# Row-wise value products for the second query block, a masked level and a halved last tile in a two-layer hybrid trunk

## The chip, the cores and the metric

The kernel runs on one core of one Trainium2 chip. A core has five engines: TensorE (PE, the matrix products; its weight loads are shown as PEld), VectorE (DVE), ScalarE (ACT), GpSimd (POOL) and SyncE (SP, which here issues the DMAs). The metric is device time in microseconds; times are medians of several runs, and a profile is one execution of its own.

## The reference

Two layers of a decoder trunk on 512 tokens of 1024 features in float32. In each layer one projection feeds four groups of four heads of 64 features:

```python
h = _rmsnorm(x, norm_g[l])
(...) = jnp.split(h @ w_in[l], split_at, axis=-1)
y = concatenate([hgrn2_mixer(...),          # gated linear recurrence, chunkwise
                 fox_mixer(...),            # softmax(q.k/8 + sums of log f), causal
                 stick_breaking_mixer(...), # A[t,s] = beta[t,s] prod(1 - beta[t,j])
                 nsa_mixer(...)])           # compressed + selected + window branch, gated
yh = y per head * rsqrt(mean(y*y) + EPS)
x = x + (yh * out_norm_g[l] * silu(gate)) @ w_out[l]
...
return _rmsnorm(x, final_norm_g)
```

In the attention groups a block of 128 queries sees the keys of its own and all earlier blocks, so query block 0 has one key block, block 1 two, block 3 four. In the first group, o[t] is a sum over s up to t of q[t] exp(b[t] - b[s]) k[s] v[s], with b the running sum of log f.

## The kernel before

All operations are recorded first (every instruction stands under the recorder's line, L484), then `Program.order` places them by a list schedule with its own costs, and they are issued in that order, one program for each engine. What sets the order are tables at the end of the file: `TIMES` (start and step of each of eight threads of work), `LEAD` and `LAG` (shifts of priority by buffer), `RESERVE` (buffers kept back), `FILL`. The engines then run their programs in order and wait for each other by semaphores.

PE's results go to four kinds of buffers: `pin` (4, projections), `pss` (2, scores and grams), `pso` (1, value products), `psm` (1, transposes of probabilities and small products).

Projections (`tproj`, `nproj`) split both operands into a high and a low part (`whi`, `wlo`, `hth`, `htl`) and add three products for each of eight chunks of 128 features, 512 output columns wide, into a `pin` buffer. They fill most of PE's time; the attention work is threaded between them.

Attention in `fox` and `stick` runs per pair of heads `i` and query block `qb`: scores, probabilities, `turned` (PE transposes them by blocks into `psm`, and VectorE or ScalarE copies them out). The value product has two forms. In the first block (`qb == 0`) it is made by rows: the turned probabilities (128 x 128) are the weights, the values (128 x 64) move, and the output already has queries on partitions. In later blocks it is a bundle (`together`, issued without anything in between) with the values as weights, the two heads on the two halves of the array, 128 probability columns moving; the output is by features, and `heads_back` copies it with ScalarE (`oT`) and transposes it back on PE. `attend` (the gated group) has only the second form, for all blocks, with two branches on the two halves and two heads moving (256 columns), and two transposes per pair. A PE product in float32 is two passes, and the trace shows each pass as a record.

The first group (`hgrn`) builds its matrix within a 128-row block by levels of width 1, 2, 4, 8, 16, 32, 64: VectorE, ScalarE and GpSimd make operand `G` (buffers `h4`, shown as `h_h`), PE makes 64 small products in one bundle per level (`gram`). Levels up to 8 multiply 32 x 32 squares, and VectorE copies the entries of that level under a mask (`copy_predicated`) into `A32`. Level 16 multiplies 16 x 16 squares, and ScalarE copies them into their place in `A32`, eight copies for each layer. GpSimd then copies `A32` into the full matrix `Ad`.

At the end `out_proj` makes the output tiles by 128 rows and halves of 512 columns, adds the old rows, and sums their squares; `final` computes the row scale (VectorE, then a power on GpSimd), scales the two halves on VectorE and ScalarE, and stores them. The last tile's second half is the last product on PE.

Of the kernel before, what the change touches and what calls it, by code (L numbers as in the profile page):

```python
# [12 lines left out]
F32 = mybir.dt.float32  # L13
# [14 lines left out]
NCMP = 31  # L28
SMALL = (8, 4, 2, 1)
O_HGQ, O_HGF, O_HGI = 0, 256, 512  # L30
# [517 lines left out]
def trunk(ctx: ExitStack, tc: tile.TileContext, cst, x, norm_g, w_in, lbl, fox_fb, pe_k, w1_k, w2_k,  # L548
# [99 lines left out]

    def nproj(w, n, tb):
        hi, lo = w  # L650
        ps = pin.tile([P, T], F32, name="pin", tag="pin")
        o = ps[:, :n]
        sl = slice(tb * P, (tb + 1) * P)
        for c in range(KC):
            pe.matmul(o, hth[:, c, sl], hi[c][:, :n], start=(c == 0), stop=False)
            pe.matmul(o, hth[:, c, sl], lo[c][:, :n], start=False, stop=False)
            pe.matmul(o, htl[:, c, sl], hi[c][:, :n], start=False, stop=(c == KC - 1))
        return o
# [124 lines left out]
    for l in range(nl):  # L783
# [257 lines left out]
        def hgrn():  # L1041
# [55 lines left out]
            for i in range(2):  # L1097
                state(i)
                yield
            for wv in SMALL[::-1] + (16, 32, 64):  # L1100
                G = h4.tile([P, 2, T], F32, name="hG", tag="h4")
# [81 lines left out]
        def fox(i):  # L1183
            need(("fx", i))
            Q1, Q2, K1, K2 = st["fx", i]
            for qb in range(NB):
# [32 lines left out]
        def stick(i):  # L1219
            need(("sb", i))  # L1220
            Q1, K1, K2 = st["sb", i]
            for qb in range(NB):
# [23 lines left out]
                po = pso.tile([P, P], F32, name="po", tag="pso")  # L1246
                if qb == 0:
                    pn = po.rearrange("p (h d) -> p h d", h=2)
                    for s in range(2):
                        pe.matmul(pn[:, s], aT[s][:, 0], bv[:, 0, 2 * i + s, :], start=True, stop=True)  # L1250
                else:
# [10 lines left out]
        def attend(qb):  # L1262
# [35 lines left out]
            for i in range(2):  # L1298
                us = {}
                for s in range(2):  # L1300
# [7 lines left out]
                    yield  # L1308
                po = pso.tile([P, 2, P], F32, name="po", tag="pso")
# [5 lines left out]
                with pr.together("pe", 0.5):  # L1315
                    for kb in range(qb + 1):
                        for br in range(2):
                            pe.matmul(po[64 * br:64 * br + 64], nv[:, kb, br, :], pT[kb][:, 2 * br:2 * br + 2],
                                      start=(kb == 0), stop=(kb == qb))
                oT = t2.tile([P, 2, P], F32, name="oT2", tag="k1", bufs=3)  # L1320
                act.activation(oT, po, AF.Copy)
                pn = pso.tile([P, 2, 2, HD], F32, name="pon", tag="pso")
                for s in range(2):
                    pe.transpose(pn[:, s], oT[:, s], ident)
                w = den[:, 1:3, 2 * i:2 * i + 2]
# [38 lines left out]
        def out_proj(w, tb, g):  # L1364
# [12 lines left out]
            if l < nl - 1:  # L1377
                wr[tb, g] = sp.dma_start(xdst[rs, cs], XY[:, tb, cs])

        def final(tb):  # L1380
# [60 lines left out]
        if not last:  # L1441
            w_hgi = wload(w_in[l + 1], [(O_HGI, 256, 0), (O_FXV, 256, 256)], 512)
        for tb in range(NB):
            out_proj(wo, tb, 1)
            if last:
# [10 lines left out]

TIMES = ((2.577, 1.29), (10.591, 0.713), (11.607, 0.725), (20.2, 0.497), (50.852, 0.974), (58.753, 0.235), (13.999, 1.112), (62.9, 0.953))
RESERVE = {'gp_G': 1, 'pin_pin': 2, 'sm_mr': 3, 't2_t2': 1, 'vp_vp': 3, 'psm_psm': 2, 'wp_whi': 2}
FILL = (0, 1, 2, 6, 3, 4, 5, 7)
LEAD = {'pin_pin': 20, 'psm_psm': -20, 'pss_pss': 10, 'qk_qk': 100, 'sm_mr': -80, 't2_k1': 120, 'vp_vp': -180, 'wp_wlo': 290, 'pa_junk': 0, 't2_t2': 0, 't2_oT': 40, 'gp_G': 10, 'pa_pa': 10, 'sm_nm': -10, 'one_htl': 100, 'one_hth': -20, 'wp_whi': 20}  # L1460
FULL = (128, 128)
# [36 lines left out]
```

## Time and profile before

| | us |
|---|---|
| median of 3 runs | 669.25 |
| lowest, highest | 668.04, 673.2 |
| the profiled execution | 669.13 |
| its span, first to last instruction | 667.3 |
| PE busy in it | 652.6 |
| VectorE, ScalarE, GpSimd busy | 464.8, 415.5, 149.8 |

The span is from the first to the last instruction; the time of the execution has 1.83 us around it. PE's granted clock is 0.995 of full speed over the span. Busy time of PE counts overlapping products as one stretch, so the distance between starts says more about what a product costs.

### The profile page before, as it was taken

How to read it: one execution, taken by the hardware profiler on the slowest of the kernel's cores; microseconds unless marked ns; L12 is line 12 of the kernel's file. 1: busy time of each engine (PE TensorE's matmuls, PEld its weight loads, DVE VectorE, ACT ScalarE, POOL GpSimd, SP SyncE). 2: the span in 40 equal slices, each digit the busy share in tenths (PEclk: the TensorE clock that was granted, in tenths of full speed). 3: DMA queues.
4: the chain of work that ended last, by engine and by line, in shares of the span. 5: the costliest groups of instructions: out<-in, count | busy, mean ns of one | idle time of the engine just before them, and what ended most of it. 6: DMA issues, size and time to landing. Idle time of an engine off the chain costs nothing.

```text
span 667.3 us, 13759 instructions
## 1 busy us (share of the span) xinstructions
PE 652.6 (98%) x5371; PEld 517.6 (78%) x5371; DVE 464.8 (70%) x968; ACT 415.5 (62%) x902; POOL 149.8 (22%) x173
## 2 busy tenths in 40 slices
PE   7999998999999999999999999999999999999996
PEld 4888986778887777777888898877788877787774
DVE  5646589667788968755672476976678898796553
ACT  5456356566766879765353655557587678886632
POOL 5000223312343313210000030350222332141000
PEclk8999999999999999999999999999999999999998
DMA  7544243451433204204352425337123411050022
GB/s 251 151 107 131 61 134 104 107 117 32 127 95 97 80 1 137 71 1 158 111 158 58 106 64 142 100 81 188 35 74 105 129 50 40 25 163 20 32 80 94
DMA packets 67161, 63.67 MB, mean 95 GB/s; under 512 B 20484, under 2 KB 51736, under 8 KB 67096
## 3 DMA queue, kind: packets, MB, share of 16 engines
q1 hardware_dynamic: 67096, 62.80, 33.1%
q8 instruction: 42, 0.69, 0.4%
q14 instruction: 23, 0.19, 0.1%
HBM read 52.79 MB, written 4.19 MB: 85 GB/s over the span
## 4 chain that ended last, share of the span: by engine, by line
PE 95%; issue 2%; DVE 1%; DMA 1%; ACT 0%; SPq 0%; POOLq 0%; POOL 0%; DVEq 0%
PE pin_pin L484 67%; PE pss_pss L484 13%; PE pso_pso L484 9%; PE psm_psm L484 7%; DMA one_XY<-in_x 1%; DVE sm_vcm L484 0%; DVE sm_K1c L484 0%; SPq L484 0%; ACT t_t L484 0%; DVE wp_wlo L484 0%; DVE h_h L484 0%; ACT pa_pa L484 0%; ACT h_h L484 0%; DVE one_XY L484 0%; POOLq L1494 0%
## 5 line engine op out<-in xcount | busy, mean ns | idle before, releaser
L484 PE MATMUL pin_pin<-wp_whi,one_hth 128*128 128x512 f32 (+1 forms) x384 | 151.9, 396 | 2.0 <-ACT wp_whi L484 2.0
L484 PE MATMUL pin_pin<-wp_wlo,one_hth 128*128 128x512 f32 (+1 forms) x384 | 151.4, 395 | 0.5 <-DVE wp_wlo L484 0.5
L484 PE MATMUL pin_pin<-wp_whi,one_htl 128*128 128x512 f32 (+1 forms) x384 | 151.0, 397 | 0.0
L484 DVE TENSOR_TENSOR wp_wlo<-wp_raw,wp_whi 128x1024 fp32r<-128x1024 f32 (+1 forms) x80 | 95.5, 1199 | 48.1 <-ACT wp_whi L484 47.9
L484 PE MATMUL pin_pin<-one_htl,wp_whi 128*128 128x512 f32 x256 | 103.0, 402 | 1.5 <-issue 1.5
L484 PE MATMUL pin_pin<-one_hth,wp_wlo 128*128 128x512 f32 x256 | 103.8, 405 | 0.0
L484 PE MATMUL pin_pin<-one_hth,wp_whi 128*128 128x512 f32 x256 | 102.8, 402 | 0.0
L484 ACT ACTIVATE wp_whi<-wp_raw 128x1024 fp32r<-128x1024 f32 (+1 forms) x80 | 82.7, 1038 | 29.8 <-PE pin_pin L484 22.7
L484 POOL TENSOR_TENSOR sm_rs<-sm_ssv,one_mhalf 128x2 f32<-128x2 f32 (+1 forms) x48 | 43.2, 901 | 204.6 <-DVE sm_ssv L484 200.6
L484 PEld LDWEIGHTS pin_pin<-wp_whi,one_hth 128*128 128x128 f32 x384 | 72.5, 189 | 13.8 <-ACT wp_whi L484 2.3
L484 PEld LDWEIGHTS pin_pin<-wp_whi,one_htl 128*128 128x128 f32 x384 | 72.5, 189 | 12.9 <-issue 1.5
L484 PEld LDWEIGHTS pin_pin<-wp_wlo,one_hth 128*128 128x128 f32 x384 | 72.7, 189 | 12.5 <-DVE wp_wlo L484 0.7
L484 PE MATMUL pss_pss<-qk_qk,qk_qk 128*128 128x512 f32 (+3 forms) x224 | 65.1, 376 | 0.0
L484 ACT ACTIVATE t_t<-pss_pss,sm_nm 128x128 f32<-128x128 f32 (+3 forms) x96 | 50.3, 527 | 21.2 <-DVE sm_nm L484 18.3
L484 PEld LDWEIGHTS pin_pin<-one_htl,wp_whi 128*128 128x128 f32 x256 | 48.1, 188 | 12.4 <-issue 2.4
L484 PEld LDWEIGHTS pin_pin<-one_hth,wp_wlo 128*128 128x128 f32 x256 | 48.2, 188 | 11.2 <-issue 1.1
L484 PEld LDWEIGHTS pin_pin<-one_hth,wp_whi 128*128 128x128 f32 x256 | 48.2, 188 | 10.1 <-issue 0.3
L484 ACT ACTIVATE pa_pa<-pa_pa 128x512 f32<-128x512 f32 (+4 forms) x90 | 50.8, 565 | 7.1 <-DVE pa_pa L484 5.7
L484 DVE TENSOR_REDUCE sm_nm<-pss_pss 128x1 f32<-128x384 f32 (+3 forms) x72 | 42.8, 597 | 16.7 <-PE pss_pss L484 16.1
L484 PE MATMUL psm_psm<-one_c_ident,t_t 128*128 128x128 f32 x320 | 53.5, 275 | 0.9 <-DVE sm_vcm L484 0.9
L484 POOL TENSOR_TENSOR h_h<-h_h,h_h 128x512 f32<-128x512 f32 (+1 forms) x16 | 26.2, 1641 | 118.0 <-ACT h_h L484 110.9
L484 ACT ACTIVATE t_t<-psm_psm 128x512 f32<-128x512 f32 (+3 forms) x72 | 38.7, 538 | 18.0 <-PE psm_psm L484 17.6
(183 smaller groups left out, 1047.7 us busy)
## 6 DMA issues: line engine op xcount, KB each, us to landing
wp_raw<-in_w_in SPq DMA_DIRECT2D x56, 256.0 KB, 3.4
wp_raw<-in_w_in SPq DMA_DIRECT2D x28, 512.0 KB, 3.7
wp_raw<-in_w_out SPq DMA_DIRECT2D x16, 512.0 KB, 3.6
qk_qk<-qk_qk SPq DMA_DIRECT2D x16, 256.0 KB, 3.4
one_XY<-in_x SPq DMA_DIRECT2D x4, 512.0 KB, 7.8
pa_pa<-in_x SPq DMA_DIRECT2D x8, 256.0 KB, 3.2
xres<-one_XY SPq DMA_DIRECT2D x8, 256.0 KB
pa_pa<-xres SPq DMA_DIRECT2D x8, 256.0 KB, 3.5
```

Of the source, the lines that this page charges most:

```text
L484: fn(*[r(a) for a in args], **{k: r(v) for k, v in kw.items()})
```

## The change

Five edits. In `fox` and `stick` the second query block (`qb == 1`) takes the row form too: four products of 64 columns (two heads, two key blocks) in place of a bundle of four, a ScalarE copy and a transpose. In `attend` the first block takes the row form: four products in place of a bundle of two, a ScalarE copy of 256 columns and two transposes. Level 16 joins the levels that multiply 32 x 32 squares and are copied under a mask; the eight ScalarE copies for each layer go, and two masked VectorE copies come. The last output tile's second half is made in two halves of 256 columns by a function of its own, `out_last`. The tables that set the order get other numbers.

```diff
-SMALL = (8, 4, 2, 1)
+SMALL = (16, 8, 4, 2, 1)
...
-            for wv in SMALL[::-1] + (16, 32, 64):
+            for wv in SMALL[::-1] + (32, 64):
...
-                for e, ps in enumerate(gram(G, G, wv if wv >= 16 else 0)):
-                    if wv >= 16:
+                for e, ps in enumerate(gram(G, G, wv if wv >= 32 else 0)):
+                    if wv >= 32:
                         for j in range(P // (2 * wv)):
                             rows_ = slice(2 * wv * j, 2 * wv * j + wv)
-                            dst = A32[e][rows_, :, 16:32] if wv == 16 else Ad[e][rows_, :, 2 * wv * j + wv:2 * wv * (j + 1)]
-                            act.activation(dst, ps[rows_], AF.Copy)
+                            act.activation(Ad[e][rows_, :, 2 * wv * j + wv:2 * wv * (j + 1)], ps[rows_], AF.Copy)
...
-                if qb == 0:
+                if qb < 2:
                     pn = po.rearrange("p (h d) -> p h d", h=2)
                     for s in range(2):
-                        pe.matmul(pn[:, s], pT[0, s], fv[:, 0, 2 * i + s, :], start=True, stop=True)
+                        for kb in range(qb + 1):
+                            pe.matmul(pn[:, s], pT[kb, s], fv[:, kb, 2 * i + s, :], start=(kb == 0), stop=(kb == qb))
...
+                if qb == 0:
+                    pn = pso.tile([P, 2, 2, HD], F32, name="pon", tag="pso")
+                    for s, br in itertools.product(range(2), range(2)):
+                        pe.matmul(pn[:, s, br], pT[0][:, 2 * br + s], nv[:, 0, br, :], start=True, stop=True)
+                else:
...
+        def out_last(w):
...
+            for u in range(2):
+                us, cs = slice(256 * u, 256 * u + 256), slice(512 + 256 * u, 768 + 256 * u)
+                dve.tensor_tensor(XY[:, tb, cs], nproj(w, 256, tb, 256 * u), old[:, us], OP.add)
+                act.activation(old[:, us], XY[:, tb, cs], AF.Square, accum_out=sq[:, u:u + 1])
+                dve.tensor_tensor(o[:, cs], XY[:, tb, cs], nxt["gb"][:, cs], OP.mult)
+                if u == 0:
+                    dve.tensor_tensor(sq[:, 2:3], sq[:, 0:1], part, OP.add)
+                    dve.tensor_scalar(sq[:, 2:3], sq[:, 2:3], 1.0 / D, EPS, op0=OP.mult, op1=OP.add)
+            dve.scalar_tensor_tensor(sq[:, 2:3], sq[:, 1:2], 1.0 / D, sq[:, 2:3], op0=OP.mult, op1=OP.add)
+            rsq(sq[:, 3:4], sq[:, 2:3], 1)
+            for us, e in ((slice(0, 640), dve), (slice(640, 1024), act)):
+                if e is act:
+                    act.activation(o[:, us], o[:, us], AF.Copy, scale=sq[:, 3:4])
+                else:
+                    dve.tensor_scalar(o[:, us], o[:, us], sq[:, 3:4], None, op0=OP.mult)
+                sp.dma_start(out[rs, us], o[:, us])
...
-RESERVE = {'gp_G': 1, 'pin_pin': 2, 'sm_mr': 3, 't2_t2': 1, 'vp_vp': 3, 'psm_psm': 2, 'wp_whi': 2}
+RESERVE = {'gp_G': 1, 'pin_pin': 2, 'sm_mr': 3, 't2_t2': 1, 'vp_vp': 1, 'psm_psm': 2, 'wp_whi': 2}
```

The same edit as in `fox` stands in `stick`, with `aT[s][:, kb]` and `bv`. `out_last(wo)` takes the place of `out_proj` and `final` for the last tile. In `TIMES`, `LEAD` and `RESERVE` six numbers differ and one is new.

What moves, at three places. First PE just ahead of level 16's bundle in the first layer, whose products are the last row (`pss` from `h_h`); `pin` products belong to a gate's projection, and `psm` ones turn probabilities `t_t`. Before:

```order
L484 MATMUL pin_pin_125<-one_hth_68,wp_wlo_99 128x512
L484 MATMUL pin_pin_125<-one_hth_68,wp_whi_104 128x512
L484 MATMUL pin_pin_125<-one_htl_69,wp_whi_104 128x512
L484 MATMUL pin_pin_125<-one_hth_68,wp_wlo_99 128x512
L484 MATMUL psm_psm_71<-one_c_ident_72,t_t_8_90 128x128
L484 MATMUL pin_pin_122<-one_hth_68,wp_whi_105 128x512
L484 MATMUL psm_psm_71<-one_c_ident_72,t_t_0_82 128x128
L484 MATMUL pss_pss_96<-h_h_4_79 16x16
```

Now:

```order
L484 MATMUL pin_pin_122<-one_hth_68,wp_wlo_100 128x512
L484 MATMUL pin_pin_122<-one_hth_68,wp_whi_105 128x512
L484 MATMUL pin_pin_122<-one_htl_69,wp_whi_105 128x512
L484 MATMUL pin_pin_122<-one_hth_68,wp_wlo_100 128x512
L484 MATMUL psm_psm_71<-one_c_ident_72,t_t_8_90 128x128
L484 MATMUL pin_pin_122<-one_hth_68,wp_whi_105 128x512
L484 MATMUL psm_psm_71<-one_c_ident_72,t_t_0_82 128x128
L484 MATMUL pss_pss_96<-h_h_4_79 32x32
```

The same two transposes stand ahead of the bundle, but 31 PE records lie between the end of level 8's bundle and this one where there were 21 (in the second layer 31 and 21 too), and counted from the program's start the bundle stands 18 instructions later (20 in the second layer; a load and a product of each pass count one each).

Second PE at the compressed keys of the gated group, first layer: `psm` from `sm_w` and `sm_hid` is the product whose result VectorE copies to `vcm`, and the `psm` transposes of `t_t` are the next to use that buffer. Before:

```order
L484 MATMUL psm_psm_71<-sm_w_0_168,sm_hid_167 128x64
L484 MATMUL pso_pso_156<-t_t_5_87,vp_vp_121 64x128
L484 MATMUL pso_pso_156<-t_t_3_85,vp_vp_121 64x128
...
L484 MATMUL pso_pso_156<-t_t_5_87,vp_vp_121 64x128
L484 MATMUL pso_pso_156<-t_t_3_85,vp_vp_121 64x128
L484 MATMUL pss_pss_96<-qk_qk_140,qk_qk_138 128x384
L484 MATMUL psm_psm_71<-one_c_ident_72,t_t_0_82 128x128 x2
```

Now:

```order
L484 MATMUL psm_psm_71<-sm_w_0_168,sm_hid_167 128x64
L484 MATMUL pss_pss_95<-qk_qk_140,qk_qk_138 128x512
L484 MATMUL pin_pin_125<-one_htl_69,wp_whi_106 128x512
L484 MATMUL pso_pso_156<-one_c_ident_72,t_oT_166 128x128
L484 MATMUL pin_pin_125<-one_hth_68,wp_wlo_101 128x512
L484 MATMUL pin_pin_125<-one_hth_68,wp_whi_106 128x512
L484 MATMUL pin_pin_125<-one_htl_69,wp_whi_106 128x512
L484 MATMUL pin_pin_125<-one_hth_68,wp_wlo_101 128x512
L484 MATMUL pin_pin_122<-wp_whi_107,one_hth_68 128x512
L484 MATMUL pin_pin_122<-wp_wlo_102,one_hth_68 128x512
L484 MATMUL psm_psm_71<-one_c_ident_72,t_t_7_89 128x128 x2
```

The bundle of value products (`pso` from `vp`) stood between the two and now stands ahead of both; eight 512-column products and a transpose stand between instead. (In the second layer the rows are alike.)

Third VectorE at the end of the program (`XY` is the sum with the old rows, `xrs` the row scale of a tile). Before:

```order
L484 TENSOR_TENSOR one_XY_67<-pin_pin_124,pa_pa_114 128x512
L484 TENSOR_TENSOR h_h_2_77<-one_XY_67,h_h_3_78 128x512
L484 TENSOR_REDUCE sm_xrs_93<-sm_xss_80 128x1
L484 TENSOR_SCALAR sm_xrs_93<-sm_xrs_93 128x1
L484 TENSOR_SCALAR h_h_2_77<-h_h_2_77,sm_xrs_93 128x512
L484 TENSOR_TENSOR one_XY_67<-pin_pin_125,pa_pa_112 128x512
L484 TENSOR_TENSOR h_h_4_79<-one_XY_67,h_h_3_78 128x512
L484 TENSOR_REDUCE sm_xrs_94<-sm_xss_80 128x1
L484 TENSOR_SCALAR sm_xrs_94<-sm_xrs_94 128x1
L484 TENSOR_SCALAR h_h_4_79<-h_h_4_79,sm_xrs_94 128x512
```

Now:

```order
L484 TENSOR_REDUCE sm_xrs_93<-sm_xss_80 128x1
L484 TENSOR_SCALAR sm_xrs_93<-sm_xrs_93 128x1
L484 TENSOR_TENSOR one_XY_67<-pin_pin_122,pa_pa_114 128x256
L484 TENSOR_SCALAR h_h_3_78<-h_h_3_78,sm_xrs_93 128x512
L484 TENSOR_TENSOR h_h_0_75<-one_XY_67,h_h_2_77 128x256
L484 TENSOR_TENSOR sm_xrs_0_177<-sm_xrs_0_177,sm_xss_80 128x1
L484 TENSOR_SCALAR sm_xrs_0_177<-sm_xrs_0_177 128x1
L484 TENSOR_TENSOR one_XY_67<-pin_pin_125,pa_pa_114 128x256
L484 TENSOR_TENSOR h_h_0_75<-one_XY_67,h_h_2_77 128x256
L484 SCALAR_TENSOR_TENSOR sm_xrs_0_177<-sm_xrs_0_177 128x1
L484 TENSOR_SCALAR h_h_0_75<-h_h_0_75,sm_xrs_0_177 128x640
```

The last sum is two of 256 columns, the reduction behind it is gone, and one scaling-and-adding instruction stands in its place; the first half's sum comes ahead of the scaling of the tile before.

## Rows read from the trace of the kernel before

**Rows 1.** The page, part 1: busy us of each engine, share, instructions.
```profile
PE 652.6 (98%) x5371; PEld 517.6 (78%) x5371; DVE 464.8 (70%) x968; ACT 415.5 (62%) x902; POOL 149.8 (22%) x173
```

**Rows 2.** Timeline of PE (start, length, operation, idle before), level 16.
```profile
111.93 1.31 PE L484 MATMUL pss_pss<-h_h 64*16 64x16 f32 x128
...
116.05 0.33 PE L484 MATMUL pso_pso<-vp_vp,t_t 128*128 128x64 f32 x2 [2.21 <-issue]
...
436.34 1.33 PE L484 MATMUL pss_pss<-h_h 64*16 64x16 f32 x128
...
440.51 0.50 PE L484 MATMUL pin_pin<-one_htl,wp_whi 128*128 128x512 f32 x1 [1.50 <-issue]
```

**Rows 3.** PE's waits: releaser, us in total, times, longest.
```profile
PE psm_psm L484 <- DVE sm_vcm L484: 0.9, 2, 0.5
```

**Rows 4.** Timeline of the last stretch, the work behind PE's last product.
```profile
660.76 0.69 DVE L484 TENSOR_TENSOR one_XY<-pin_pin,pa_pa 128x512 f32<-128x512 f32 x1 [2.63 <-PE pin_pin L484]
661.48 0.63 ACT L484 ACTIVATE pa_pa<-one_XY 128x512 f32<-128x512 f32 x1 [3.12 <-DVE one_XY L484]
...
662.24 0.15 DVE L484 TENSOR_REDUCE sm_xrs<-sm_xss 128x1 f32<-128x2 f32 x1
...
662.66 0.54 POOL L484 TENSOR_TENSOR sm_xrs<-sm_xrs,one_mhalf 128x1 f32<-128x1 f32 x1 [5.06 <-DVE sm_xrs L484]
...
663.24 0.49 DVE L484 TENSOR_SCALAR h_h<-h_h,sm_xrs 128x512 f32<-128x512 f32 x1 [0.66 <-POOL sm_xrs L484]
```

**Rows 5.** Timeline of PE around a second block's value products.
```profile
203.78 0.40 PE L484 MATMUL pin_pin<-one_hth,wp_whi 128*128 128x512 f32 x1
204.02 0.40 PE L484 MATMUL pin_pin<-one_htl,wp_whi 128*128 128x512 f32 x1
204.34 0.66 PE L484 MATMUL pso_pso<-t_t,vp_vp 128*64 128x128 f32 x8
...
205.50 0.39 PE L484 MATMUL pin_pin<-one_htl,wp_whi 128*128 128x512 f32 x1
205.73 0.27 PE L484 MATMUL pso_pso<-one_c_ident,t_oT 128*128 128x128 f32 x1
...
206.07 0.39 PE L484 MATMUL pin_pin<-one_hth,wp_whi 128*128 128x512 f32 x1
```

**Rows 6.** Timeline of PE around a first block's value products.
```profile
198.53 0.55 PE L484 MATMUL pso_pso<-vp_vp,t_t 128*128 128x64 f32 x4
...
199.21 0.40 PE L484 MATMUL pin_pin<-one_hth,wp_wlo 128*128 128x512 f32 x1
```

**Rows 7.** Timeline of PE, gated attention's first block.
```profile
576.27 0.65 PE L484 MATMUL pso_pso<-t_t,vp_nv 128*64 128x256 f32 x4
```

**Rows 8.** Groups of PE by form (times, busy us, mean ns): the 32-wide grams.
```profile
L484 PE MATMUL pss_pss<-h_h 64*32 64x32 f32 x1152 | 11.9, 200 | 0.0
```

**Rows 9.** Groups of VectorE and ScalarE by form, 256 columns.
```profile
L484 DVE TENSOR_TENSOR t_k<-pso_pso,sm_nden 128x256 f32<-128x256 f32 x24 | 10.0, 419 | 12.2 <-PE pss_pss L484 6.5 <-PE pso_pso L484 5.7
L484 DVE COPY_PREDICATED t_k<-one_c_u,pss_pss 128x256 f32<-128x256 uint8 x16 | 6.2, 442 | 0.3
...
L484 ACT ACTIVATE t_t<-t_k 128x256 f32<-128x256 f32 x8 | 3.3, 415 | 5.0 <-DVE t_k L484 4.1 <-POOL t_k L484 0.9
```

**Rows 10.** Timeline of VectorE, its product for level 16, first layer.
```profile
110.22 1.45 DVE L484 TENSOR_TENSOR h_h<-h_h,h_h 128x512 f32<-128x512 f32 x1
```

**Rows 11.** The page, part 3: packets, MB and time share of a DMA queue.
```profile
q8 instruction: 42, 0.69, 0.4%
```

**Rows 12.** Timeline of PE at the compressed keys, first layer.
```profile
214.99 0.43 PE L484 MATMUL psm_psm<-sm_w,sm_hid 64*128 64x64 f32 x2
...
217.37 0.41 PE L484 MATMUL psm_psm<-one_c_ident,t_t 128*128 128x128 f32 x2 [0.55 <-DVE sm_vcm L484]
```

**Rows 13.** Timeline of PE, 256-column products in attention.
```profile
118.40 0.71 PE L484 MATMUL pss_pss<-qk_qk,qk_qk 128*128 128x256 f32 x4
...
118.95 0.40 PE L484 MATMUL pin_pin<-one_htl,wp_whi 128*128 128x512 f32 x1
```

More of the change, by code (lines that the diff above doesn't have):

```diff
@@ L647, in tproj, with nproj @@
         return ps
-    def nproj(w, n, tb):
+    def nproj(w, n, tb, c0=0):
         hi, lo = w
@@ L654, in nproj @@
         for c in range(KC):
-            pe.matmul(o, hth[:, c, sl], hi[c][:, :n], start=(c == 0), stop=False)
-            pe.matmul(o, hth[:, c, sl], lo[c][:, :n], start=False, stop=False)
-            pe.matmul(o, htl[:, c, sl], hi[c][:, :n], start=False, stop=(c == KC - 1))
+            pe.matmul(o, hth[:, c, sl], hi[c][:, c0:c0 + n], start=(c == 0), stop=False)
+            pe.matmul(o, hth[:, c, sl], lo[c][:, c0:c0 + n], start=False, stop=False)
+            pe.matmul(o, htl[:, c, sl], hi[c][:, c0:c0 + n], start=False, stop=(c == KC - 1))
         return o
@@ L1246, in stick @@
                 po = pso.tile([P, P], F32, name="po", tag="pso")
-                if qb == 0:
+                if qb < 2:
                     pn = po.rearrange("p (h d) -> p h d", h=2)
                     for s in range(2):
-                        pe.matmul(pn[:, s], aT[s][:, 0], bv[:, 0, 2 * i + s, :], start=True, stop=True)
+                        for kb in range(qb + 1):
+                            pe.matmul(pn[:, s], aT[s][:, kb], bv[:, kb, 2 * i + s, :], start=(kb == 0), stop=(kb == qb))
                 else:
@@ L1308, in attend @@
                     yield
-                po = pso.tile([P, 2, P], F32, name="po", tag="pso")
                 pT = []
@@ L1314, in attend @@
                         yield
[L1315 to L1324, printed above, removed]
+                if qb == 0:
[3 more added lines that the diff above has]
+                else:
+                    po = pso.tile([P, 2, P], F32, name="po", tag="pso")
+                    with pr.together("pe", 0.5):
+                        for kb in range(qb + 1):
+                            for br in range(2):
+                                pe.matmul(po[64 * br:64 * br + 64], nv[:, kb, br, :], pT[kb][:, 2 * br:2 * br + 2],
+                                          start=(kb == 0), stop=(kb == qb))
+                    oT = t2.tile([P, 2, P], F32, name="oT2", tag="k1", bufs=3)
+                    act.activation(oT, po, AF.Copy)
+                    pn = pso.tile([P, 2, 2, HD], F32, name="pon", tag="pso")
+                    for s in range(2):
+                        pe.transpose(pn[:, s], oT[:, s], ident)
                 w = den[:, 1:3, 2 * i:2 * i + 2]
@@ L1378, in out_proj @@
                 wr[tb, g] = sp.dma_start(xdst[rs, cs], XY[:, tb, cs])
+        def out_last(w):
+            tb, o = NB - 1, nxt["xg"][NB - 1]
+            rs = slice(tb * P, (tb + 1) * P)
+            old = pa.tile([P, 512], F32, name="old", tag="pa")
+            ld = sp.dma_start(old, xsrc[rs, 512:1024])
+            if (tb, 1) in xwr:
+                pr.after(ld, xwr[tb, 1])
+            sq = sm.tile([P, 4], F32, name="xrs4", bufs=1)
+            part = nxt["xss"][:, tb, 0:1]
+            for u in range(2):
[14 more added lines that the diff above has]
+                sp.dma_start(out[rs, us], o[:, us])
         def final(tb):
@@ L1443, in trunk @@
         for tb in range(NB):
+            if last and tb == NB - 1:
+                out_last(wo)
+                break
             out_proj(wo, tb, 1)
@@ L1454, in trunk @@
     pr.issue(ctx, tc, order)
-TIMES = ((2.577, 1.29), (10.591, 0.713), (11.607, 0.725), (20.2, 0.497), (50.852, 0.974), (58.753, 0.235), (13.999, 1.112), (62.9, 0.953))
-RESERVE = {'gp_G': 1, 'pin_pin': 2, 'sm_mr': 3, 't2_t2': 1, 'vp_vp': 3, 'psm_psm': 2, 'wp_whi': 2}
+TIMES = ((2.577, 1.29), (10.591, 0.713), (11.607, 0.725), (20.2, 0.497), (50.852, 0.974), (58.753, 0.329), (12.483, 1.112), (62.9, 0.907))
+RESERVE = {'gp_G': 1, 'pin_pin': 2, 'sm_mr': 3, 't2_t2': 1, 'vp_vp': 1, 'psm_psm': 2, 'wp_whi': 2}
 FILL = (0, 1, 2, 6, 3, 4, 5, 7)
-LEAD = {'pin_pin': 20, 'psm_psm': -20, 'pss_pss': 10, 'qk_qk': 100, 'sm_mr': -80, 't2_k1': 120, 'vp_vp': -180, 'wp_wlo': 290, 'pa_junk': 0, 't2_t2': 0, 't2_oT': 40, 'gp_G': 10, 'pa_pa': 10, 'sm_nm': -10, 'one_htl': 100, 'one_hth': -20, 'wp_whi': 20}
+LEAD = {'pin_pin': 20, 'psm_psm': -20, 'pss_pss': 10, 'qk_qk': 0, 'sm_mr': -80, 't2_k1': 120, 'vp_vp': -180, 'wp_wlo': 290, 'pa_junk': 0, 't2_t2': 0, 't2_oT': 40, 'gp_G': 20, 'pa_pa': 10, 'sm_nm': -10, 'one_htl': 100, 'one_hth': -20, 'wp_whi': 20, 'h4_h4': -20}
 FULL = (128, 128)
```

## The prediction

> **What bounds the kernel now.** I read the page's engine line first: TensorE (PE) is busy for 652.6 of 667.3 us, so whatever an edit takes off other engines can count only within the 14.7 us in which PE stands still [rows 1]. Then PE's timeline, to see where those 14.7 us lie: at the two ends of the program, in two stretches of 2.21 and 1.50 us in which PE waits for nothing that the trace names [rows 2], and in two waits of 0.9 us together for VectorE's copies of `vcm` [rows 3]. Elsewhere PE runs practically without a gap. So three things can move the time: PE's own work, these few stops, and the chain behind PE's last product [rows 4]. Busy time does not price PE's work, since matmuls overlap in it; I take distances between starts instead. A 512-column product takes 0.234 us from start to start (203.78 to 204.02, as in the long runs of them) [rows 5].
>
> **Value products of the second block, 8 of them** (two head pairs, fox and stick, two layers). Now: a bundle of eight records on halves of the array, a ScalarE copy, one transpose back. From 203.78 to 206.07 PE does the bundle, the transpose and six 512-column products; 2.29 less 6 x 0.234 leaves 0.886 us for the two [rows 5]. Afterwards: four products with the probabilities as weights, eight records of the kind that the first block already has. There four records and one 512-column product take 199.21 - 198.53 = 0.68 us, so 0.446 for the four, 0.111 each, and 0.89 for eight [rows 6]. The edit costs PE 8 x (0.89 - 0.886) = **0.0 us**: the bundle with its transpose, and the row form without one, take the same. The ScalarE copies that go were hidden: PE shows no wait for them.
>
> **Gated attention, first block, 4 of them.** Its bundle's row is 0.65 us long, like the other bundle's 0.66 [rows 5, 7], so I give it the same price without a transpose. A transpose costs 206.07 - 205.50 - 2 x 0.234 = 0.10 [rows 5], which leaves 0.78; with the two transposes here 0.98, against 0.89 for eight row records: 4 x -0.09 = **-0.4 us**.
>
> **Level 16 under a mask.** PE issues the same 128 records per layer; nine groups of the 32-wide form take 11.9 us, 1.32 each, and the 16-wide ones 1.31 and 1.33 [rows 2, 8]: **0**. VectorE gets two masked copies of 0.44 us per layer [rows 9] and ScalarE loses eight small ones. The masked copies are hidden as long as the next level's operands come in time; if that cover went they would cost 4 x 0.44 = 1.8 us. VectorE's product for level 16 ended only 0.26 us before PE needed it (110.22 + 1.45 against 111.93) [rows 2, 10], so this is where I expect trouble if there is any. The new order speaks against it: between the bundles of level 8 and level 16 stand 31 PE records where there were 21, and behind level 16 there are still 49 records before level 32.
>
> **The two unnamed stops.** PE's 10,742 loads and products came in 42 packets of queue q8, 256 to a packet [rows 1, 11]. Counted in the order of before, the two stops lie 5,377 instructions apart, which is 21 blocks of 256 and one: both fall on a block's end. One block earlier lies 6 instructions into the first level 16 bundle and 14 into the second, at about 111.96 and 436.41; PE runs on at 116.05 and 440.51, 4.1 us later both times [rows 2]. So I read them as the wait for the next block of code, asked for at one block's end and needed at the next, which a bundle of 256 instructions brings within 1.3 us. In the new order these bundles start 18 and 20 instructions later. The earlier block end then stands 12 and 6 instructions ahead of the bundle and the next one close to the bundle's end. In the first layer PE gets there after four 512-column products, two transposes, 95% of the bundle and about 0.3 for the change of shape and the last product's length: 0.94 + 0.2 + 1.2 + 0.3 = 2.6 us, stop 4.1 - 2.6 = 1.5. In the second after one product, two transposes and 98% of it: 0.23 + 0.2 + 1.2 + 0.3 = 1.9, stop 2.2. Together 3.7, as now (2.21 + 1.50): **0**. Bounds: both gone, -3.7; both at 2.6, +1.5.
>
> [...]
>
> **Waits for `vcm`.** In both layers the transposes of `t_t` wait until VectorE has emptied the one `psm` buffer: in the first layer they start 2.38 us after the product before them in that buffer (214.99 to 217.37), and 0.55 of it is waiting; both layers together 0.9 [rows 3, 12]. In the new order eight 512-column products and one transpose stand between, 8 x 0.234 + 0.1, and the product itself (its row is 0.43 long) [rows 12]: 2.3 to 2.4 us, where 2.38 sufficed. So the wait goes but for some 0.05 per layer: **-0.8 us**. Bounds: 0 (VectorE gets to those copies later) and -0.9.
>
> **Last output tile in halves.** Each half has 24 products of 256 columns. The nearest rows are four of attention's 256-column products in 118.95 - 118.40 = 0.55 us, 0.14 each with what is left of the mask ahead of them [rows 13]; from below, half of 0.234. I take 0.12: 48 x 0.003 = **+0.1 us** (bounds 0 and 48 x 0.023 = +1.1). Behind PE's last product stand now VectorE's sum, ScalarE's square, a reduction and a scaling of one number, GpSimd's power, the last scaling [rows 4]; then only the second half's chain does. The sum goes from 0.69 to 0.42 and the square from 0.63 to 0.42 (256-column rows) [rows 4, 9]; reduction and scaling (662.24 to 662.66, 0.42) become one instruction, about 0.2. That is 0.27 + 0.21 + 0.2 = 0.7. The last scaling is cut 640 to 384: VectorE's 0.49 for 512 becomes about 0.57, and its store is issued first, so 0.1 is given back: **-0.6 us**. Bounds -0.8 and 0 (as many bytes as now have to land at the end).
>
> **Sum.** 0.0 - 0.4 + 0 + 0 - 0.8 + 0.1 - 0.6 = -1.7 us against the profiled execution's 669.13 (span 667.3 and 1.83 around it), which is next to the median of 669.25: **667.4 us**, a quarter of a per cent less. A measurement of this kernel tells about 1% (6.7 us) from no change, so the forecast is "the same".
>
> **Rivals.**
> [...]
> *The new order opens waits as large as those it closes.* Slack is thin in places (0.26 us at level 16), and the two layers have the same order, so a wait comes twice: 0.45 us, the mean of the `vcm` waits, at two places per layer gives 1.8, hence 669.2.
> *Slower: levels late on VectorE.* The bundle of level 4 now comes about 1.4 us sooner (14 records behind level 2 instead of 20). If VectorE does not keep that pace, the bundles of levels 8 and 16 wait for their own product, up to 1.45 us each in two layers [rows 10]: 4 x 1.45 = 5.8, and 673.2. It decides from where VectorE's share of a level, with the added copies, passes the PE time between two bundles. For it: only 0.26 us of slack at level 16. Against it: levels 8 and 16 have more PE work ahead of them than now, not less.
>
> **How the numbers follow.** Forecast 0.64 (666 to 668.7); code stops gone 0.08; waits opened as closed 0.16; levels late 0.08; something unseen and clearly slower 0.04. The range 664.0 to 670.6 takes in the forecast with its bounds, nearly all of the first two rivals and about what the runs spread below and above their middle; it leaves out the slow ones. Faster by over 1% needs under 662.6, more than all named gains with both code stops gone: 0.03. Slower by over 1% needs over 675.9: 0.05. The rest, 0.92, is within 1%.
>
> **What would show it.** Right: records of the row products at 0.111 us; no bundle of eight in the second block; PE idle without a named cause in or right behind both level 16 bundles, about 1.5 and 2.2 us; no wait of over 0.1 us for `vcm`; from VectorE's last sum to the last scaling's end 0.6 us less than now (660.76 to 663.73) [rows 4]. Wrong: rows in PE's waits that name `h_h` (the levels) or copies of `t_t`; 256-column products in the last tile at over 0.13 us; or unnamed stops away from the ends of code blocks, which would undo my reading of them.

## The result, and the profile after

The changed kernel takes **673.48 us** (median of 16 runs, 672.24 to 677.12) against 669.32 of the kernel before on the same chips (16 runs, 668.04 to 673.2): a ratio of 1.0063, interval 1.0052 to 1.0074. It is slower by 4.2 us, where 1.7 us less had been forecast. The profiled execution is the longest of the 16 (677.12 us, span 675.3), so I take sizes from it and then ask which of them the other runs share.

The page of the changed kernel, the engines' busy time and the granted clock in 40 slices:

```profile
PE 658.7 (98%) x5395; PEld 527.6 (78%) x5395; DVE 469.1 (69%) x975; ACT 408.6 (61%) x876; POOL 147.2 (22%) x173
...
PEclk8999999799999999999999999999999999999999
```

TensorE (PE) is still the bound, with 6.1 us more of busy time than before [rows 1], and the eighth slice of its clock has fallen below full speed. PE's waits in the changed kernel (total, times, longest):

```profile
PE pss_pss L484 <- issue: 3.9, 2, 2.4
PE pss_pss L484 <- DVE t_k L484: 1.8, 2, 0.9
PE pin_pin L484 <- ACT wp_whi L484: 1.8, 1, 1.8
PE pss_pss L484 <- DVE h_h L484: 1.4, 1, 1.4
PE psm_psm L484 <- DVE one_ones L484: 1.0, 1, 1.0
PE psm_psm L484 <- DVE sm_vcm L484: 0.4, 1, 0.4
PE pso_pso L484 <- DVE one_XY L484: 0.2, 1, 0.2
```

New is the second line: two waits for `t_k`, the masked copies. The unnamed stops are still there (3.9 after 3.71 [rows 2]), the waits for `vcm` have halved [rows 3]. The places in PE's timeline, changed kernel:

```profile
108.84 1.29 PE L484 MATMUL pss_pss<-h_h 64*32 64x32 f32 x128
...
112.35 0.27 PE L484 MATMUL pss_pss<-one_c_bf 128*128 128x256 bf16 x1 [0.85 <-DVE t_k L484]
...
117.70 1.24 PE L484 MATMUL pss_pss<-h_h 64*32 64x32 f32 x122
121.33 0.33 PE L484 MATMUL pss_pss<-h_h 64*32 64x32 f32 x6 [2.38 <-issue]
...
211.09 1.00 PE L484 MATMUL pso_pso<-vp_vp,t_t 128*128 128x64 f32 x8
211.90 0.48 PE L484 MATMUL pin_pin<-one_htl,wp_whi 128*128 128x512 f32 x1
...
441.75 0.27 PE L484 MATMUL pss_pss<-one_c_bf 128*128 128x256 bf16 x1 [0.93 <-DVE t_k L484]
...
447.11 1.26 PE L484 MATMUL pss_pss<-h_h 64*32 64x32 f32 x125
449.91 0.25 PE L484 MATMUL pss_pss<-h_h 64*32 64x32 f32 x3 [1.54 <-issue]
```

The bundle at 108.84 is level 8, those at 117.70 and 447.11 are level 16 (now 32 columns wide). The scores' mask product at 112.35 needs one of the two `pss` buffers, both of which level 8 has filled and VectorE must copy out. What VectorE did meanwhile, with one row of GpSimd, changed kernel:

```profile
107.97 0.68 DVE L484 TENSOR_TENSOR h_h<-h_h,h_h 128x512 f32<-128x512 f32 x1
...
109.27 1.28 POOL L484 TENSOR_TENSOR h_h<-h_h,h_h 128x512 f32<-128x512 f32 x1 [2.38 <-ACT h_h L484]
109.39 1.70 DVE L484 TENSOR_TENSOR h_h<-h_h,h_h 128x512 f32<-128x512 f32 x1
111.13 0.69 DVE L484 SCALAR_TENSOR_TENSOR qk_qk<-pin_pin,qk_qk 64x512 fp32r<-64x512 f32 x1
111.85 0.78 DVE L484 COPY_PREDICATED t_k<-one_c_u,pss_pss 128x256 f32<-128x256 uint8 x2
```

The bundle is done at 110.1, but a product and a q/k split stand ahead of the copies, which start only at 111.85. At the end of the first stop the clock falls; windows of the changed kernel (length, busy us and count of PE, PEld, VectorE, ScalarE and GpSimd, then PEclk, the share of DMA and GB/s):

```profile
117.00:121.00 4.00, 1.95 (x127) 1.48 (x126) 2.03 (x4) 0.99 (x2) 0.00 (x0) 1.00 0.56 171
121.30:128.00 6.70, 6.67 (x27) 5.32 (x27) 3.98 (x8) 1.33 (x2) 5.44 (x10) 0.50 0.31 79
```

The granted clock is 0.50 for these 6.7 us where it was 1.00 until then, and 512-column products stand 0.43 us apart in them (126.28 to 126.71) for 0.234; by my estimate up to half of it, 3.4 us, is lost. The tail behind PE's last product, changed kernel:

```profile
669.00 0.28 PE L484 MATMUL pin_pin<-wp_whi,one_htl 128*128 128x256 f32 x1
669.31 0.42 DVE L484 TENSOR_TENSOR one_XY<-pin_pin,pa_pa 128x256 f32<-128x256 f32 x1 [1.39 <-PE pin_pin L484]
669.77 0.42 ACT L484 ACTIVATE pa_pa<-one_XY 128x256 f32<-128x256 f32 x1 [2.28 <-DVE one_XY L484]
...
670.31 0.16 DVE L484 SCALAR_TENSOR_TENSOR sm_xrs<-sm_xrs 128x1 f32<-128x1 f32 x1
670.55 0.54 POOL L484 TENSOR_TENSOR sm_xrs<-sm_xrs,one_mhalf 128x1 f32<-128x1 f32 x1 [4.40 <-DVE sm_xrs L484]
...
671.13 0.55 DVE L484 TENSOR_SCALAR h_h<-h_h,sm_xrs 128x640 f32<-128x640 f32 x1 [0.66 <-POOL sm_xrs L484]
```

From the sum's start to the scaling's end on VectorE 2.37 us pass, where 2.97 did [rows 4].

For what follows I call **the stretch** the time from the start of PE's 39th record behind the warm-up (at about 20 us, with the granted clock back at 1.00) to the start of its last product. It is 641.41 us before and 648.05 after. The new order has three 512-column products fewer and three transposes of 0.109 us more ahead of that record, so between the two orders some 0.4 us of the difference comes from the mark alone. So of the 8.0 us between the two profiled executions 2.0 lie ahead of the stretch (the first product starts at 12.48 instead of 10.85, and the clock stays at 0.50 until 18.8 instead of 15.4), 6.6 in it, and -0.7 in the tail.

### The profile page after: what moved, and what is told of

It reads as the page before. It is cut to its first block, busy times and chain, and to the rows that moved or that the text cites. A ratio compares the mean times of both kernels' runs of the same rounds, so it can differ in the third digit from the quotient of the medians.

```text
span 675.3 us, 13801 instructions
## 1 busy us (share of the span) xinstructions
PE 658.7 (98%) x5395; PEld 527.6 (78%) x5395; DVE 469.1 (69%) x975; ACT 408.6 (61%) x876; POOL 147.2 (22%) x173
## 4 chain that ended last, share of the span: by engine, by line
PE 90%; DVE 5%; issue 2%; DMA 1%; ACT 1%; SPq 0%; POOL 0%; POOLq 0%; DVEq 0%
PE pin_pin L484 63%; PE pss_pss L484 12%; PE pso_pso L484 9%; PE psm_psm L484 6%; DVE h_h L484 1%; DVE pa_pa L484 1%; DMA one_XY<-in_x 1%; DVE qk_qk L484 1%; ACT pa_pa L484 0%; DVE t_k L484 0%; DVE sm_vcm L484 0%; ACT t_t L484 0%; SPq L484 0%; DVE one_XY L484 0%; DVE sm_K1c L484 0%
## 5 line engine op out<-in xcount | busy, mean ns | idle before, releaser
L484 PE MATMUL pin_pin<-wp_whi,one_hth 128*128 128x512 f32 (+2 forms) x392 | 153.6, 394 | 1.8 <-ACT wp_whi L484 1.8
L484 PE MATMUL pin_pin<-wp_wlo,one_hth 128*128 128x512 f32 (+2 forms) x392 | 154.0, 394 | 0.0
L484 PE MATMUL pin_pin<-wp_whi,one_htl 128*128 128x512 f32 (+2 forms) x392 | 153.1, 392 | 0.0
L484 PEld LDWEIGHTS pin_pin<-wp_whi,one_hth 128*128 128x128 f32 x392 | 74.4, 190 | 13.4 <-ACT wp_whi L484 2.0
L484 PEld LDWEIGHTS pin_pin<-wp_whi,one_htl 128*128 128x128 f32 x392 | 74.4, 190 | 12.6 <-issue 1.5
L484 PEld LDWEIGHTS pin_pin<-wp_wlo,one_hth 128*128 128x128 f32 x392 | 74.4, 190 | 11.1 <-DVE wp_wlo L484 0.3
L484 DVE TENSOR_REDUCE sm_nm<-pss_pss 128x1 f32<-128x384 f32 (+3 forms) x72 | 42.8, 597 | 11.9 <-PE pss_pss L484 8.2
L484 PEld LDWEIGHTS psm_psm<-one_c_ident,t_t 128*128 128x128 f32 x320 | 39.8, 141 | 11.8 <-issue 1.9
```

What stands on the lines that cost most here:

```text
L484: fn(*[r(a) for a in args], **{k: r(v) for k, v in kw.items()})
```

## The experiments

None of these kernels leaves out any of the computation. "Before" was run again beside each group: 669.91, 669.26, 669.35 and 669.54 us.

**Tables alone, edits alone.** The change is three tables (TIMES, RESERVE, LEAD) and the edits; each was run without the other.

```
order_alone: before.py with the changed TIMES, RESERVE, LEAD
edits_alone: after.py with the old TIMES, RESERVE, LEAD
```

> The kernel before with the three tables of the change and none of its edits. Theory (the new order is what costs, the edits are worth what was forecast, about -0.9 us together: gated first block -0.4, last tile -0.5): 673.5 + 0.9 = 674.4 us, PE waits twice for the masked copies of level 8 (about 0.9 us each), and the two unnamed stops behind the level 16 bundles stay at 2.4 and 1.5 us, since those bundles start at almost the same places of the program. Rival (the edits cost, above all the masked level 16 on VectorE): 669 to 670, no wait for the masked copies.

Measured: 675.32 us, ratio 1.0086 (1.0072 to 1.0100); waits for the masked copies 1.8, unnamed stops 4.6, and further waits (`nden` 1.3, `t_oT` 0.7, `t_t` 0.5).

> The changed kernel with the three tables of before. Theory (the order costs): the edits alone give 669.3 - 0.9 = 668.4 us, with waits for vcm and code stops as before (2.2 and 1.5) and no wait for masked copies. Rival (the edits cost): 672 to 674 and waits of PE for masked copies or for h_h.

Measured: 671.52 us, ratio 1.0024 (1.0010 to 1.0039); no wait for masked copies, stops 2.4 and 1.4, in place of `vcm` waits of 1.3 for `htl` and 1.0 for `t_t`, and a clock of 0.50 for 3.4 us behind the first stop (window 116.7 to 120.0). The order costs, as the theory said, but the edits under the old tables cost 1.6 us as well: a planner that is fed other instructions makes another list, and its waits are part of the edit.

**Where the bundles lie against the blocks of code.** Cutting warm-up products into narrower ones moves everything behind by whole instructions and changes no order. In shift24 (the changed kernel) four of the 22 products become four of 128 columns each; in shift216 (the changed kernel) 18 of them, and in before_s228 (the kernel before) 19, become seven of 73 columns each, by the same kind of edit. The added lines of shift24:

```
+        for k in range(n):
+            o = pe.matmul(pz, zero, ..., start=True, stop=True)
+            if n == WARM[0] and k < 4:
+                o.call = lambda: [nc.tensor.matmul(pz[:, P * j:P * j + P].real(), zero.real(), zero.real(), start=True, stop=True)
+                                  for j in range(NB)]
```

> The changed kernel in which four of the 22 warm-up products are each cut into four of 128 columns: the same columns, 24 more TensorE instructions ahead of everything, and the same order behind. The level 16 bundles of 256 instructions then start some 24 instructions later against the blocks of code. Theory (the unnamed stops are waits for the next block of 256 instructions): both stops go, 2.4 + 1.5 = 3.9 us less, 669.6 us, and 3 us less again in those executions where the stop is followed by a low granted clock. Rival (the stops belong to the level 16 rows or to what follows them): they stay at the same instructions, 673.5 us.

Measured: 673.66 us, ratio 1.0060 (1.0046 to 1.0074), no gain. The first layer's stop in shift24, timeline of PE:

```profile
115.56 1.14 PE L484 MATMUL pss_pss<-h_h 64*32 64x32 f32 x110
118.57 0.30 PE L484 MATMUL pss_pss<-h_h 64*32 64x32 f32 x18 [1.88 <-issue]
```

The stop moved from behind 122 records of the bundle to behind 110. A record is a weight load and a product, so that is 24 instructions: the stop is tied to a count of instructions from the start of the program, not to a row. In the kernels of all seven profiles with unnamed stops, PE's first stop stands behind the same 2,481st load or product (1,241 loads and 1,240 products before, and as many in the changed kernel). That bears out the block's end. The traces also show the code arriving: it comes in packets of 16,384 bytes on queue q8, 42 of them for the 10,742 loads and products before, 256 to a packet [rows 1, 11], and ahead of each of the fourteen stops in these seven profiles one such packet lands 1.3 to 1.6 us before PE runs on. For the first stop of the changed kernel, the DMA view of the window 118.6 to 120.0 us (packets, MB, time share), with PE running on at 121.33:

```profile
q8 instruction: 1, 0.02, 6.0%
```

My rule for when a stop is gone failed: with 36 instructions (some 4 us) between the earlier block end and the bundle I expected none. So I moved the end behind the bundle:

> The changed kernel in which 18 of the 22 warm-up products are each cut into seven (the same columns, 216 TensorE instructions more). The blocks of 256 then end 29 and 34 instructions behind the level 16 bundles instead of 3 and 9 records ahead of their end, so that some 14 ordinary products (3.3 us) stand between bundle and boundary. Theory (the stops are waits for the next block of code, and only where a bundle takes most of a block's last 192 instructions): both stops fall under 0.5 us, 3 us less; the granted clock has no low stretch in the middle of the program, 1.5 us less on the mean of the runs: 669 us. The warm-up may run longer for its many weight loads, up to 1 us. Rival (the stops belong to these rows and only move inside them, as they did by 12 records under a shift of 24): 3.9 us of unnamed stops again, 673.5.

Measured: **668.32 us**, 5.2 less than the changed kernel, ratio to before 0.9976 (0.9961 to 0.9992). Waits of PE in shift216; no unnamed stop is left, and the waits for `t_k` stand as before:

```profile
PE pin_pin L484 <- ACT wp_whi L484: 2.7, 1, 2.7
PE pss_pss L484 <- DVE t_k L484: 1.8, 2, 0.9
...
PE psm_psm L484 <- DVE sm_vcm L484: 0.4, 1, 0.4
```

The 192 instructions in that theory were my estimate, and no run shows them. The runs show stops with 220 and 226 of a bundle's instructions ahead of the block's end (shift24), and none with the end 29 and 34 instructions behind the bundles.

> The kernel before with 19 of its 22 warm-up products cut into seven (228 TensorE instructions more), nothing else. The block ends then lie 35 and 42 instructions behind its level 16 bundles. Theory: the stops of 2.2 and 1.5 us go, 669.6 - 3.5 = 666 us. Rival: they stay, 669.6.

Measured: **666.25 us**, ratio 0.9949 (0.9928 to 0.9970), no unnamed stop. The stretch falls from 641.41 to 637.84, by 3.57 for stops of 3.71. In the changed kernel it falls from 648.05 to 640.77, by 7.28: 3.9 of stops and 3.4, by my estimate, of the low clock. Over all runs the mean granted clock is 0.992 after, 0.995 in shift216, 0.994 before; that mean counts the low stretches at the start and the end of the program too (in the kernel before 0.50 from 11.9 to 15.4 us and from 663.9 on).

**The masked copies of level 8.** VectorE's two copies (marked `hoist` where they are recorded) are put ahead of the product and the split; PE's order stays.

```
     order = pr.order()
+    for o in pr.ops:
+        if getattr(o, "hoist", False):
+            order.remove(o.idx)
+            order.insert(max(order.index(j) for j in o.deps) + 1, o.idx)
     pr.issue(ctx, tc, order)
```

> The changed kernel with VectorE's two masked copies of level 8 put ahead of its product for level 16 and of one q/k split, in both layers; the order of TensorE is unchanged. Theory (PE waits twice 0.9 us there for the scores' buffer that these copies empty, since they stand behind 2.4 us of VectorE work that has time): the two waits go and with them 2.2 us, 671.2 us; no new wait for h_h at level 16, whose bundle comes 6 us later. Rival (the product is late in their place): PE waits for h_h at level 16 or for the pin buffer, 673.5.

Measured: 674.70 us, ratio 1.0068 (1.0047 to 1.0089). The two waits are gone, yet nothing is gained: the unnamed stops grow from 3.9 to 4.9 (by my reading because PE comes to the blocks' ends sooner), and the mean clock of the runs is 0.989.

> Both edits at once on the changed kernel: masked copies of level 8 ahead, and the 216 instructions of warm-up. Theory: the two gains add, 673.5 - 2.2 - 4.4 = 667 us, below the kernel before. Rival (one of them is no cause): 669 to 671.

Measured: 668.70 us, ratio 0.9982 (0.9966 to 0.9998), no less than shift216. The stretch is 0.7 shorter (640.05), not 2.2. Waits of PE in this kernel:

```profile
PE pss_pss L484 <- DVE h_h L484: 2.1, 2, 1.7
...
PE pso_pso L484 <- DVE t_t L484: 0.5, 2, 0.3
```

1.7 of the first line is at the start of the program; the other 0.4, for level 8's own operand in the second layer, and the 0.5 for copies of `t_t` behind level 16 are new. VectorE's lateness moves on to the next thing it is asked for, so taking these waits out of the changed kernel gave back 0.7 us of 1.8.

So the wait was put, alone, into the kernel before:

```
# late8: before_s228, VectorE's order in both layers
+ TENSOR_TENSOR wp_wlo<-wp_raw,wp_whi 128x1024
  COPY_PREDICATED t_k<-one_c_u,pss_pss 128x256   (two, level 8)
- TENSOR_TENSOR wp_wlo<-wp_raw,wp_whi 128x1024
```

> The kernel before under 228 more warm-up instructions (666.25 us), with one step of VectorE moved in both layers: the split of a weight chunk (1.21 us) stands ahead of the two masked copies of level 8 and no longer behind them; every other engine's order is the same. Theory (the main cost of the new order is that VectorE empties the scores' buffer late, whatever the work ahead of it): PE waits about 0.9 us for the masked copies in either layer, as in the changed kernel, and the time is 2 us more, 668.3. Rival (the wait is paid back by the slack behind it, and the new order's cost lies elsewhere): 666.3 to 666.8.

Measured: **668.86 us**, 2.6 more than before_s228 (666.25), ratio 0.9989 (0.9976 to 1.0002). VectorE and PE in late8, first layer:

```profile
110.17 1.23 DVE L484 TENSOR_TENSOR wp_wlo<-wp_raw,wp_whi 128x1024 fp32r<-128x1024 f32 x1 [0.22 <-issue]
111.43 0.78 DVE L484 COPY_PREDICATED t_k<-one_c_u,pss_pss 128x256 f32<-128x256 uint8 x2
...
111.92 0.27 PE L484 MATMUL pss_pss<-one_c_bf 128*128 128x256 bf16 x1 [1.15 <-DVE t_k L484]
```

One step of VectorE on the wrong side of two copies lengthens the stretch by 2.20 (637.84 to 640.04), with PE's order untouched. None of it is paid back later.

**Edits and tables again, clear of the stops.**

```
edits_s228: edits_alone + 228 instructions;  order_s216: order_alone + 216
```

> The edits alone (the three tables of before), with 19 warm-up products cut into seven so that the level 16 bundles are clear of the blocks' ends. Theory: of the 1.6 us that the edits alone lost, the part behind the stops (a low granted clock of 3.4 us in the profile, mean clock 0.993) goes, and what is left is the new list's waits (1.3 us for htl and 1.0 for t_t in place of 0.9 for vcm) less 0.9 us of the edits: 666.7 us, next to the kernel before under the same shift (666.25). Rival (the edits cost TensorE or VectorE more by themselves): 668 us or more.

Measured: 667.67 us, ratio 0.9969 (0.9952 to 0.9987), between theory and rival. Its stretch is 639.78, 1.9 above before_s228, with the same waits for `htl` and `t_t` as in edits_alone.

> The tables alone (none of the edits), with 18 warm-up products cut into seven. Theory: the order itself costs by waits that have nothing to do with the blocks of code (1.8 us for the masked copies, 1.3 for nden, 0.7 + 0.5 for copies ahead of psm) and more changes of shape on TensorE; only its two stops of 4.6 us go: 675.3 - 4.6 = 670.7 us, 4.5 above the kernel before under its shift. Rival (what the order costs is where it puts the bundles against the blocks): 666 to 667 us.

Measured: 674.09 us, ratio 1.0058 (1.0039 to 1.0077). The rival falls, and my number too: the stretch lost 3.5 us (648.84 to 645.30) with its stops, but waits of 0.5 for `t_k` on ScalarE and 0.6 more for `nden` came up, and the stretch began 1.8 later (20.20 for 18.42). The tables without the edits cost 7.5 us of stretch (0.4 of it the mark). On the edited list they show no gain either: with them and clear of stops the stretch is 640.77 (shift216), without them 639.78 (edits_s228).

**The mask.**

```
nomask16 / nomask_s216: after.py (+216 instructions) with
-SMALL = (16, 8, 4, 2, 1)
+SMALL = (8, 4, 2, 1)
... and the lines for level 16 as in before.py (eight ScalarE copies)
```

> The changed kernel and its tables, but level 16 goes back to eight ScalarE copies per layer in place of two masked copies on VectorE. Theory (PE's waits at level 8 come from the new order, which asks for the scores' buffer right behind the level 8 bundle, ahead of level 16): they stay, twice 0.9 us, and the time is 673.5 within 0.5. Rival (the two masked copies more per layer make VectorE late): the waits go and the time falls by 2 to 671.3 us.

Measured: 675.58 us, ratio 1.0087 (1.0073 to 1.0101): slower, not the same, but with a mean clock of 0.989 and the waits for `t_k` in place (1.7). So again without stops:

> The changed kernel with level 16 back on ScalarE, under the 216 instructions of warm-up, beside the changed kernel under the same (668.3 us). Theory (the masked copies of level 16 lie beside other work; the 2.1 us by which their removal was slower came from the low clock behind the stops, 0.989 on the mean of those runs): 668.3 within 0.5. Rival (the mask itself is worth about 2 us under the new order): 670.4.

Measured: 669.56 us, ratio 0.9998 (0.9983 to 1.0013), 1.2 more than shift216, and 1.0 more of stretch. Waits of PE in nomask_s216 that shift216 has not:

```profile
PE pss_pss L484 <- ACT t_k L484: 0.5, 2, 0.3
```

The eight small copies hold the scores' buffer too, so the mask is worth about 1 us here. In the kernel before this wait doesn't show: with its stops gone it appears (0.4 in before_s228), so the stop had covered it.

**The last tile alone, and a version that beats both.**

```
before_s228_tail: before_s228 + out_last and nproj(..., c0) of the change
before_fwarm_tail: the same edit on before; warm-up of 4 float32 products (64 columns of weights) for 22 bf16 ones
```

> The kernel before with its 228 warm-up instructions and one edit of the change, the last output tile in two halves; the order of everything ahead of that tile is that of before. Theory: the chain behind the last product is 0.6 to 0.7 us shorter and the 48 products of 256 columns cost TensorE nothing: 666.25 - 0.65 = 665.6 us. Rival (what is gained behind the last product is lost in front of it): 666.3.

Measured: 666.33 us against 666.25: not told apart by medians of 6 and 8 runs. In the profile the tail is 0.67 shorter (6.35 for 7.02 us from the last product's start to the span's end) and the stretch 0.11 longer.

> The kernel before with its last output tile in two halves, and its 22 warm-up products replaced by four in float32 with 64 columns of weights: 28 TensorE instructions fewer, so the level 16 bundles lie against the blocks of code as under 228 more, and no 43rd block is fetched at the start. Theory: the stops are gone (-3.6), the tail is 0.65 shorter, and the first product starts as early as in the kernel before, 0.9 us ahead of the kernels with cut warm-up: 665.2 us. Rival (a shorter warm-up on half the columns leaves the clock low for longer at the start): 667 or more, with a low granted clock at the start for over 3.4 us.

Measured: **664.95 us**, ratio 0.9935 (0.9923 to 0.9948), the fastest of all. The first product starts at 10.81, as in the kernel before; the stretch is 637.99, the tail 6.35, the clock low for 3.4 us at the start (0.995 on the mean of the span, as in the kernel before).

## Why the prediction was wrong

**The step that failed** is the term "Level 16 under a mask: 0" with its reason: "The masked copies are hidden as long as the next level's operands come in time." There the sum also judges what the new order does to VectorE's copies at the levels, and it reads the 31 records for 21 as more room. The copies that cost time are not those that the mask adds at level 16 but those of level 8, which the kernel before has too. It is the order that makes them late: the tables alone show the same 1.8 us of waits, the edits alone none, and the mask by itself gains about 1 us (nomask_s216). What hides a level's masked copies is not the next level but the score products that take the same two `pss` buffers. In both orders a mask product follows the level 8 bundle, four 512-column products later before and five now. Rows of PE and VectorE in the kernel before, first layer:

```profile
106.46 1.29 PE L484 MATMUL pss_pss<-h_h 64*32 64x32 f32 x128
...
108.08 0.79 DVE L484 COPY_PREDICATED t_k<-one_c_u,pss_pss 128x256 f32<-128x256 uint8 x2
...
108.71 0.28 PE L484 MATMUL pss_pss<-one_c_bf 128*128 128x256 bf16 x1
```

Before, VectorE began the copies 0.3 us behind the bundle's end (108.08 against 107.75), now 1.7 us (111.85 against 110.13). I had counted PE's records between bundles, which gave more room than before, and not looked at who takes the buffer next and what VectorE has queued ahead of the copies. The cost was 0.85 + 0.93 us of waiting; late8 prices 2.3 us of the same waits at 2.2 us of stretch. Some 1.0 us of the lateness is the product at 109.39, which took 1.70 us beside GpSimd's where the one at 107.97 took 0.68. By my estimate from these rows the copies would have been in time without it; no run tests that. My rival of the levels late on VectorE named the engine but the wrong object (the product that PE never waited for at these levels in the changed kernel) and, at 5.8 us, too high a price.

**The code stops** came where forecast, "close to the bundle's end" (122 and 125 of 128 records), and at 2.38 + 1.54 = 3.9 us for 3.7. That the sum came out is luck: 1.5 had been forecast for the first layer and 2.2 for the second. Two things in that step were wrong. The 4.1 us [rows 2] from one block's end to PE's running on is no constant: it is 4.9 and 3.3 in the changed kernel, and in shift24 some 7 us (the 36 instructions ahead of the bundle begin at 111.5, PE runs on at 118.57). What varies is the start of the code packet: about 1.0 to 2.3 us behind the earlier block's end in twelve of the fourteen stops, 4.7 and 3.9 us in shift24. What sets it I could not settle. And a stop has a second price that I didn't have: the clock behind it. It fell from 1.00 to 0.50 for 6.8 us in the profiles of the changed kernel and nomask16 and for 3.4 us in those of edits_alone and shift24, between 0.1 us ahead of a stop's end and 1.0 us behind it. In hoist8_s216, without a stop, 512-column products keep their 0.23 us around the level 16 bundles (95 to 125 and 424 to 452). In the profile before it had stayed at 1.00 (15.4 to 663.8), so no row showed it. I estimate this at some 1.3 us of the 4.2: the mean clocks of the runs (0.992 for 0.994) give that much, and the medians of the changed kernel and shift216 differ by 5.2 us, 1.3 more than the stops. The profile after, with its 6.8 us, is at the high end.

That shifts of 228 and 216 instructions take 3.0 and 5.2 us off, and that a code packet lands 1.3 to 1.6 us ahead of PE's running on, shows that PE waits for code where a bundle takes 220 to 256 instructions of a block in 1.1 to 1.3 us.

**`vcm` waits, -0.8.** They fell from 0.9 to 0.4 (the first layer still waits 0.41), and 0.2 for `XY` came up. So the size was off by half here, and the rival of "waits as large as those it closes" was at work beside that of the late levels.

**PE's own work.** Eight row records take 211.90 - 211.09 = 0.81 us, 0.10 each, and the 512-column product behind them 0.32 (211.90 to 212.22) where it takes 0.234 in a long run: 0.90 together for the forecast 0.89, whose 0.111 each had that product's delay in it; the last tile's 256-column products stand 0.117 apart, just half of a 512-column one, so the +0.1 was nothing. **The tail** gave -0.6 to -0.7, as forecast.

**The sum as measured.** Stretch without stops +2.9 (640.77 - 637.84), larger stops +0.2, low clock +1.3 by the estimate above, tail -0.7: 3.7 for the 4.2 of the medians, or 3.3 without the 0.4 that the mark puts into the stretch. In the 2.9 are 1.8 of waits for the masked copies, -0.8 of other named waits (`vcm`, `XY`, and ScalarE's `t_k`, which before_s228 has), the 0.4 of the mark, and some 1.5 us by which the distances between PE's starts grew without a named wait. The cause of that last part stays open; the gated group's forecast -0.4 was not read by itself.

## What to carry to other kernels

Before an order is changed, follow each shared buffer from the bundle that fills it to the next taker, and read what the emptying engine has queued ahead of the copies; the distance between two bundles on the busy engine says nothing of that. Where a bundle of tiny products runs through a block of code as fast as here (256 instructions in 1.3 us), count instructions: a shift of the whole program by some 220 instructions was worth 3 to 5 us here, more than any edit. And price a planner's tables and the edits together, since either alone cost more than its parts promised.

## What the runs showed of the hardware

- An unnamed stop of PE of 1.4 to 2.6 us at the end of a 256-instruction block (10,742 loads and products in 42 packets [rows 1, 11]), when 110 to 128 records of the bundle fall just ahead of it; none when the block ends 28 to 187 instructions behind a bundle (all other bundles of the sixteen profiles). PE runs on 1.3 to 1.6 us after a 16,384-byte code packet has landed (fourteen stops).
- A stop of that length can be followed by a granted clock of 0.50 for 6.8 us (changed kernel, nomask16) or 3.4 us (edits_alone, shift24), or by none (before: 1.00 from 15.4 to 663.8 us). How often it is in the other runs is not shown: they left only a mean clock over the whole span (0.989 to 0.994 in the 16 runs after).
- VectorE's product of two 128x512 operands takes 0.68 us alone and 1.70 while GpSimd does the same kind of product beside it (107.97 against 109.39, GpSimd from 109.27). Where the two overlap for less, it takes less: 0.80 us with 0.25 us of overlap, 1.32 with 0.77 (kernel before).
- Kernels with 216 or 228 instructions more in the warm-up, at practically the same columns, start the first product at 11.8 to 12.8 us instead of mostly 10.8 to 11.5. They have a 43rd packet of code, and their first one comes at 8.4 to 9.1 us, otherwise after 20 (23.4 before, 25.0 in the changed kernel).
